# Spreading a batch norm's scale and shift over partitions: VectorE turns and quadrant copies in place of TensorE matmuls

## The chip, the core and the metric

The kernel runs on one core of one Trainium2 chip. The metric is the device time of one execution in microseconds; the time of a kernel is the median of its runs.

## The reference

A matrix product of 8192 rows (16 x 512) by 1024 by 768 columns, then a batch norm over all rows of each column, all in float32:

```python
batch, m, k, n = 16, 512, 1024, 768
...
y = np.matmul(x, weight)
mean = np.mean(y, axis=(0, 1), keepdims=True)
var = np.var(y, axis=(0, 1), keepdims=True)
y_norm = (y - mean) / np.sqrt(var + eps)
return (gamma * y_norm + beta).astype(np.float32)
```

No output can be stored until the statistics of its column over all 8192 rows are known.

## The kernel before

The 8192 rows are cut into 16 chunks of 512 (`C = 16`, `CH = 512`), the 768 columns into 6 tiles of 128 (`NT = 6`). x is read as float32 and cast to bf16 by the Pool queue's DMAs (`load_x`, L403) into a ring; VectorE turns it (`turn_x`, L435) so that k lies on partitions.

The first two column tiles (`GA = 2`, together `NA = 256` columns) are computed in two ways. For chunks 0 to 13 the product has **rows on partitions** (`mm_rows`, L510): sums and squares are added up in the tiles `sum1`, `sum2` and `sum3`, and a bf16 copy of y is kept. For the last two chunks (`RC = 14`) it has **columns on partitions** (`ga_unit`, L814), with statistics by VectorE. The other four tiles have columns on partitions throughout (`mm`, L575), each with its own pass over the chunks; some of those passes' work is already done while x still arrives.

When all chunks of the first two tiles are through, their statistics are finished: `merge` and `more` (L795, L800) join the accumulators into `tot`; eight small matmuls (`sums_rows`, L871) sum over partitions; `sums_entry` and `aggregate_rows` (L880 to L887) give mean and variance; `root_rows` (L891) takes the root on ScalarE; `scale_rows` and `shift_rows` (L894 to L899) make scale and shift with one column on each partition. That form serves the blocks of chunks 14 and 15 (`ga_block`): VectorE normalises them in place (L1064), TensorE turns them (L1074), ScalarE copies them out of PSUM (L1082), SyncE stores them (L1085).

The blocks of chunks 0 to 13 (`rows_out`) need scale and shift along the free dimension, the same on every partition. In the kernel before, TensorE does that spread (`spread`, L903): a matmul of the scale column, broadcast, with a float32 identity, four times for scale and shift of two tiles, each of which shows as two matmuls in the profile; the results stay in two PSUM banks (`aff[0]`, `aff[1]`). `shift_sbuf` (L915) copies the shift to `sum1` for Pool, which can't read it in PSUM here. Then VectorE multiplies each block (L937), VectorE (the blocks in `ADDED`) or Pool adds the shift (both L942), and SyncE stores (L946).

While this goes on, TensorE continues with tile 2, whose statistics for chunks 4 to 15 are ScalarE's (`keep_sum` L720, `square_sum` L724), then with tiles 3, 4 and 5, whose statistics are VectorE's (L711). Three of these tiles have some blocks (`raw_block`) whose scale and shift are spread in another way: `raw_spread` makes the two columns 32 wide, turns them in 32 x 32 blocks on VectorE (L1142), gathers the four quadrants into the first one (`gather`, L1145), deals them to the other three quadrants, and keeps them in a bank (L1158).

The order of all this is not written out by hand. Every step is a `task` with a due time (`prio`), the engines that may run it with estimated costs, what it depends on, and the buffers that it takes. `arrange` simulates the engines with these estimates, and at each moment takes, among the tasks that can start, the one with the lowest due time. The order that comes out is fixed per engine when the kernel is built. TensorE can host transposes of finished blocks between the matmuls of a chunk (`hosts`). So a change of a cost or a due time can move work far from its place.

Of the kernel before, what the change touches and what calls it, by code (L numbers as in the profile page):

```python
# [227 lines left out]
def kernel(  # L228
# [19 lines left out]
    P = 128  # L248
    NT = N // P
    KQ = K // 4  # L250
    CH = 512
# [13 lines left out]
    GA = 2  # L265
    NA = GA * P
    GY = 2
    PAD = 50
    HELD = 1
    PAIRED = 1  # L270
    ASTAT = {2:tuple(range(4,16))}
    RC = C - 2
    XT, YB, SQ = C - EARLY, 28, 3
    ADDED = (0,6,16,28,40)
# [18 lines left out]
    def seq(bi):  # L293

        ins = bi.ins
        prev = last.get(ins.engine)
        if prev is not None:
            tc.add_manual_dep(
                ins, prev,
                mybir.DependencyInfo(mybir.DependencyClass.NoSync, mybir.DependencyReason.DATA),  # L300
                reason="order",
            )
        last[ins.engine] = ins.name
        return bi
# [26 lines left out]
        seq(nc.vector.memset(sums[nt][:, 1:2], float(len(ASTAT[nt]) * CH)))  # L331
    msq = singles.tile([P, GA], f32)
    gst = singles.tile([P, GA, 3 + 12 * (C - RC)], f32)
    seq(nc.vector.memset(gst, float(RC * CH)))
    ngamma = singles.tile([P, NT], f32)
    nscale = singles.tile([P, 1], f32)
# [19 lines left out]
    def task(prio, engines, emit, deps=(), lock=False, **kw):  # L356
        t = Task(prio, engines, emit, deps, **kw)
        t.lock = lock
        tasks.append(t)
        return t  # L360

    def dve(occ):
        return {"DVE": (occ, occ + 0.09)}

    def act(occ):
        return {"ACT": (occ, occ + 0.11)}

    def pool(occ):
        return {"POOL": (occ, occ + 0.05)}

    def pe(occ):
        return {"PE": (occ, occ + 0.03)}
# [73 lines left out]
    t = 1.0  # L446
# [412 lines left out]


    S = clock[0]
    tot_slot, a0_slot, a1_slot = Slot(banks), Slot(banks), Slot(banks)
    aff = {}

    def sums_rows(eng):
# [24 lines left out]
    def root_rows(eng):  # L890
        seq(nc.scalar.activation(std[:, g], mv[:, g, 1], AF.Sqrt, bias=eps_sb, scale=1.0))  # L891

    def scale_rows(eng):
        seq(nc.vector.reciprocal(std[:, g], std[:, g]))  # L894
        seq(nc.vector.tensor_mul(scale[:, g], std[:, g], gamma_sb[:, g]))

    def shift_rows(eng):
        seq(nc.vector.tensor_mul(tmp[:, g], mv[:, g, 0], scale[:, g]))
        seq(nc.vector.tensor_sub(shift[:, g], beta_sb[:, g], tmp[:, g]))  # L899

    def spread(dst, row, nt):

        seq(nc.tensor.matmul(dst, row[:, nt:nt + 1].to_broadcast([P, P]), ident32, start=True, stop=True,  # L903
                             skip_group_check=True))

    def spread_rows(i):
        def emit(eng):
            a_ps = psum.tile([P, CH], f32, tag="b")
            aff[i] = a_ps[:, 0:NA]
            for a in range(GA):  # L910
                spread(a_ps[:, a * P:(a + 1) * P], (scale, shift)[i], a)
        return emit

    def shift_sbuf(eng):
        seq(nc.scalar.copy(sum1[:, 0:NA], aff[1]))  # L915

    U = S - 30.0
    s1 = task(U, pe(0.9), sums_rows, merges, takes=[tot_slot])
    se = task(U, dve(0.8), sums_entry, [s1], True, uses=[tot_slot])
    ag = [task(U, dve(0.25), aggregate_rows(a), [se] + [h[0] for k, h in ga_half.items() if k[0] == a]) for a in range(GA)]  # L920
    rt = task(U, {"ACT": (0.2, 0.3)}, root_rows, ag)
    sc = task(U, dve(0.3), scale_rows, [rt], True)
    sr = task(U + 0.1, dve(0.35), shift_rows, [sc], True)
    p0 = task(U, pe(0.45), spread_rows(0), [sc], takes=[a0_slot])
    p1 = task(U, pe(0.45), spread_rows(1), [sr], takes=[a1_slot])
    p1.look = 0.6
    sh = task(U, act(0.3), shift_sbuf, [p1], uses=[a1_slot])


    def rows_out(c, s0, s1, k):  # L930
        due = S + 5.0 + 0.62 * k
        n = s1 - s0
        slot = Slot(rings, n * NA)

        def norm(eng):
            slot.o = piece(slot).rearrange("p (s n) -> p s n", n=NA)
            seq(nc.vector.tensor_mul(  # L937
                slot.o, y_row[c].y[:, s0:s1], aff[0][:, None, :].to_broadcast([P, n, NA])))

        def add(eng):  # L940
            row = sum1[:, 0:NA] if eng == "POOL" else aff[1]
            seq(ENG[eng].tensor_add(slot.o, slot.o, row[:, None, :].to_broadcast([P, n, NA])))  # L942

        def store(eng):
            m0 = c * CH
            seq(nc.sync.dma_start(  # L946
                out_flat[m0 + s0 * P:m0 + s1 * P, 0:NA].rearrange("(s p) n -> p s n", p=P), slot.o))

        keeps = [row_end[k][3] for k in row_end if k[0] == c]
        a = task(due, dve(0.3 * n), norm, [p0] + keeps, takes=[slot], uses=[y_row[c], a0_slot])  # L950
        b = task(due + 0.4, dve(0.3 * n) if k in ADDED else pool(0.59 * n), add, [a, p1 if k in ADDED else sh],
                 uses=[slot, a1_slot] if k in ADDED else [slot])
        task(due + 1.0, {"SP": (0.38, 0.4)}, store, [b], dma=n * NA * P * 4 / 1024 / 365.0 * 1.024,
             uses=[slot])

# [100 lines left out]
    def ga_block(c, due):  # L1056
        yslot = y_row[c]
        slot, bank = Slot(rings, RT * NA), Slot(banks)
        todo = []

        def norm_ga(a):
            def emit(eng):
                part = yslot.y[:, a]
                seq(nc.vector.tensor_scalar(  # L1064
                    part, part, scale[:, a:a + 1], shift[:, a:a + 1], op0=ALU.mult, op1=ALU.add))
            return emit

        def step():
            if not todo:
                o_ps = psum.tile([P, RT, GA, P], bf16, tag="b")  # L1070
                bank.tile = o_ps
                todo.extend((o_ps[:, s, a], yslot.y[:, a, s * P:(s + 1) * P]) for s in range(RT) for a in range(GA))
            dst, src = todo.pop(0)
            seq(nc.tensor.transpose(dst, src, ident))  # L1074

        def emit(eng):
            for _ in range(emit.task.count):
                step()

        def copy(eng):  # L1080
            slot.o = piece(slot).rearrange("p (s n) -> p s n", n=NA)
            seq(nc.scalar.copy(slot.o, bank.tile.rearrange("p s a n -> p s (a n)")))  # L1082

        def store(eng):
            seq(nc.sync.dma_start(out_flat[c * CH:(c + 1) * CH, 0:NA].rearrange("(s p) n -> p s n", p=P), slot.o))  # L1085

        emit.step = step
        norms = [task(due, dve(0.25), norm_ga(a), [sr] + [h[1] for k, h in ga_half.items() if k[1] == c], True, uses=[yslot])
                 for a in range(GA)]
        t = task(due, pe(0.0555 * RT * GA), emit, norms, takes=[bank], uses=[yslot])  # L1090
        emit.task = t
        turns[t] = [RT * GA, RT * GA]
        d = task(due, act(0.905), copy, [t], takes=[slot], uses=[bank])
        task(due, {"SP": (0.38, 0.4)}, store, [d], dma=RT * NA * P * 4 / 1024 / 365.0 * 1.024, uses=[slot])

    for c in range(RC, C):
        ga_block(c, S - 29.8 + 35.5 * (c - RC))

    def raw_turn(nt, c, due):

# [26 lines left out]
    def raw_spread(nt, fin_task):  # L1127
        bank = Slot(banks)
        k = sorted(RAW).index(nt)
        acc, at = ((sum2, 0), (sum2, 2 * P), (sum3, 2 * P))[k]  # L1130
        row = acc[:, at:at + 2 * P].rearrange("p (i n) -> p i n", n=P)
        wide, turned = sum1[:, NA + 64 * k:NA + 64 * (k + 1)], sum3[:, 64 * k:64 * (k + 1)]
        both = turned.rearrange("p (i n) -> p i n", n=32)
        now = clock[0] + RAWDUE[nt] + 2.0

        def quadrant(i):
            return slice(32 * i, 32 * i + 32)

# [24 lines left out]
        t = task(now, act(0.4), keep, [s], takes=[bank])  # L1163
        raw_aff[nt] = bank, t, s, row[:, 1]
# [247 lines left out]
```

## Time and profile before

| | us |
|---|---|
| median of 3 runs | 205.81 |
| lowest, highest | 205.71, 205.83 |
| span of the profiled execution (first to last instruction) | 204.1 |
| busy: TensorE, VectorE, ScalarE, Pool in that span | 189.3, 159.3, 146.2, 124.1 |
| HBM read, written | 36.71 MB, 25.17 MB |

The page and the trace give the profiled execution's time as its span; what lies around the span isn't recorded there separately, so it is read as the median less the span, 1.71 us. In the profile PE is TensorE, PEld its weight loads, DVE VectorE, ACT ScalarE, POOL GpSimd (Pool), SP SyncE, which issues the stores. The first x arrives at about 12 us; the statistics of the first two tiles are complete at about 106 us, and the stores begin at 109 us.

### The profile page before, as it was taken

What the parts mean: (1) busy time and instruction counts of PE and PEld (TensorE: products, weight loads), DVE (VectorE), ACT (ScalarE), POOL (GpSimd) and SP (SyncE); (2) the same over time, 40 slices, a digit from 0 to 9 for tenths busy, and PEclk for the clock granted to TensorE, in tenths of its full rate; (3) what the DMA queues carried; (4) which work ended last, traced back from release to release, by engine and by line L of the source; (5) the groups of instructions that cost most, each with busy time, mean ns of one, the idle gap of its engine ahead of it and who ended that gap; (6) DMA issues with size and microseconds to landing.
All of it is one profiled execution on the core that took longest, in us unless ns stands there. A gap on an engine that the chain in (4) does not pass through costs nothing.

```text
span 204.1 us, 3510 instructions
## 1 busy us (share of the span) xinstructions
PE 189.3 (93%) x1210; PEld 114.5 (56%) x1210; DVE 159.3 (78%) x250; ACT 146.2 (72%) x260; POOL 124.1 (61%) x150
## 2 busy tenths in 40 slices
PE   7969999999999999999999999999999999997900
PEld 3457554657488888777865444444444445544600
DVE  4031879999999999969989998987999878657900
ACT  2001461368989999899978766999998959956950
POOL 7776954877499989997403999389613312940000
PEclk9999999999999999999999999999999999999965
DMA  4999999999999999999686899899999999999998
GB/s 71 172 199 196 176 196 196 196 197 197 190 193 197 197 196 196 196 197 195 103 181 200 297 339 336 248 301 328 295 322 227 336 303 274 347 343 310 310 347 253
DMA packets 98562, 48.74 MB, mean 239 GB/s; under 512 B 24304, under 2 KB 98032, under 8 KB 98544
## 3 DMA queue, kind: packets, MB, share of 16 engines
q0 software_dynamic: 34624, 18.36, 65.5%
q1 hardware_dynamic: 63920, 30.16, 52.6%
q8 instruction: 9, 0.15, 0.3%
q14 instruction: 9, 0.07, 0.1%
HBM read 36.71 MB, written 25.17 MB: 303 GB/s over the span
## 4 chain that ended last, share of the span: by engine, by line
PE 86%; ACT 3%; DMA 3%; POOL 2%; issue 1%; ACTq 0%; DVE 0%; POOLq 0%
PE y_ps L575 54%; PE y_ps L510 24%; PE y_ps L814 4%; ACT o_sb L1361 3%; DMA ring<-in_x_dram 3%; PE o_ps L1044 1%; POOL ring L403 1%; POOL w_sb L387 1%; PE y_ps L753 1%; PE a_ps L903 1%; PE o_ps L1074 0%; ACTq L1407 0%; PE idle_ps L591 0%; PE tot_ps L871 0%; ACT ring L1252 0%
## 5 line engine op out<-in xcount | busy, mean ns | idle before, releaser
L575 PEld LDWEIGHTS <-w_sb 128*128 128x128 bf16 x520 | 50.3, 97 | 57.6
L575 PE MATMUL y_ps<-xT_sb,w_sb 128*128 128x512 bf16 (+1 forms) x272 | 59.3, 371 | 0.0
L575 PE MATMUL y_ps<-x_pl,w_sb 128*128 128x512 bf16 x248 | 57.4, 379 | 0.0
L403 POOL DMA_DIRECT2D ring<-in_x_dram x76 | 47.2, 626 | 14.4 <-DMA ring<-in_x_dram 5.5
L510 PE MATMUL y_ps<-w_sb,xT_sb 128*128 128x256 bf16 x448 | 50.6, 273 | 1.7 <-DMA ring<-in_x_dram 1.6
L510 PEld LDWEIGHTS <-xT_sb 128*128 128x128 bf16 x448 | 43.5, 98 | 9.4 <-DVE xT_sb L435 2.9
L435 DVE STREAM_TRANSPOSE xT_sb<-ring 128x1024 f32<-128x1024 f32 (+1 forms) x29 | 31.2, 1111 | 14.1 <-DMA ring<-in_x_dram 13.9
L711 DVE BATCH_NORM_STATS2 stats<-y_ps 128x6 f32<-128x512 f32 x46 | 30.9, 687 | 7.7 <-PE y_ps L575 7.2
L715 ACT CAST y_sb<-y_ps 128x512 bf16<-128x512 f32 x51 | 29.0, 593 | 10.4 <-DVE stats L711 6.3
L547 ACT COPY x_pl<-xT_sb 128x1024 bf16<-128x1024 bf16 x32 | 32.8, 1063 | 1.7 <-DVE xT_sb L435 1.7
L942 POOL TENSOR_TENSOR ring<-ring,sum 128x1024 f32<-128x1024 f32 (+1 forms) x11 | 23.8, 2188 | 14.9 <-ACT y_ps L724 10.9
L659 ACT ACTIVATE sq_sb<-y_ps 128x512 f32<-128x512 f32 x28 | 16.3, 610 | 16.2 <-PE y_ps L510 15.9
L666 POOL TENSOR_TENSOR sum<-sum,sq_sb 128x512 f32<-128x512 f32 x20 | 25.6, 1278 | 3.0 <-ACT sq_sb L659 1.7
L662 DVE TENSOR_TENSOR sum<-y_ps,sum 128x512 f32<-128x512 f32 x28 | 18.9, 675 | 6.3 <-ACT sq_sb L659 5.3
L672 ACT CAST y_sb<-y_ps 128x512 bf16<-128x512 f32 x28 | 16.3, 594 | 8.2 <-DVE sum L662 8.0
L1178 POOL TENSOR_TENSOR ring<-ring,sum 128x1024 f32<-128x1024 f32 x6 | 14.8, 2477 | 9.8 <-issue 8.5
L937 DVE TENSOR_TENSOR ring<-y_sb,a_ps 128x1024 f32<-128x1024 bf16 (+1 forms) x16 | 16.7, 1079 | 0.1
L1044 PE MATMUL o_ps<-ident,y_sb 128*128 128x128 bf16 x104 | 13.1, 221 | 1.6 <-DVE y_sb L1348 1.5
L1232 ACT CAST ring<-ring 128x1024 f32<-128x1024 bf16 x13 | 13.8, 1063 | 0.6 <-DMA ring<-y_sb 0.6
L1145 POOL COPY sum<-sum 32x256 f32<-32x256 f32 (+1 forms) x17 | 5.8, 340 | 13.4 <-DVE sum L1142 6.5
L428 DVE STREAM_TRANSPOSE xT_sb<-ring 128x2048 bf16<-128x2048 bf16 x6 | 13.5, 2290 | 0.1
L591 PE MATMUL idle_ps<-idle_sb 128*128 128x512 f32 x18 | 9.6, 688 | 1.5 <-DVE idle_sb L316 1.5
(104 smaller groups left out, 153.7 us busy)
## 6 DMA issues: line engine op xcount, KB each, us to landing
out_dram<-ring SPq DMA_DIRECT2D x37, 512.0 KB, 3.4
ring<-in_x_dram POOLq DMA_DIRECT2D x52, 256.0 KB, 8.8
out_dram<-o_sb SPq DMA_DIRECT2D x6, 512.0 KB, 4.7
ring<-in_x_dram POOLq DMA_DIRECT2D x16, 128.0 KB, 5.9
w_sb<-in_weight_dram POOLq DMA_DIRECT2D x8, 192.0 KB, 6.2
out_dram<-ring SPq DMA_DIRECT2D x6, 256.0 KB, 3.0
ring<-in_x_dram POOLq DMA_DIRECT2D x4, 192.0 KB, 7.8
out_dram<-o_sb SPq DMA_DIRECT2D x3, 256.0 KB, 2.5
```

The lines of the kernel that those rows point to most:

```text
L403: bi = seq(nc.gpsimd.dma_start(x_bf[32 * i:32 * i + 32], src[:, :, KQ * i:KQ * (i + 1)]))
L435: seq(nc.vector.transpose(dst, src[:, :, jw0:jw1]))
L510: seq(nc.tensor.matmul(y_ps[:, s], x_of(c, jw, e, t * P, (t + 1) * P), w_sb[:, jw, e, 0:NA], start=(s == 0 and jw == 0 and e == 0), stop=( ...
L547: seq(nc.scalar.copy(dst, pairs) if eng == "ACT" else ENG[eng].tensor_copy(dst, pairs))
L575: seq(nc.tensor.matmul(y_ps, w_sb[:, jw, e, nt * P:(nt + 1) * P], moving(c, jw, e, q0 * QR, q1 * QR, parted), start=(jw == 0 and e == 0 an ...
L659: seq(nc.scalar.activation(sq_sb[:, 0:n], slot.tile[:, 0:n], AF.Square))
L662: seq(nc.vector.tensor_add(sum1, slot.tile[:, 0:n], sum1))
L666: seq(ENG[eng].tensor_add(acc, acc, state["sq"][:, 0:n]))
L711: seq(nc.vector.bn_stats(dst, slot.tile))
L715: seq(nc.scalar.copy(y(nt, c), slot.tile))
L937: seq(nc.vector.tensor_mul(slot.o, y_row[c].y[:, s0:s1], aff[0][:, None, :].to_broadcast([P, n, NA])))
L942: seq(ENG[eng].tensor_add(slot.o, slot.o, row[:, None, :].to_broadcast([P, n, NA])))
```

## The change

The four spreads on TensorE, `scale_rows`, `shift_rows` and `shift_sbuf` are gone. In their place: `terms_rows` (Pool) puts gamma, 0 and beta into two small tiles; `first_rows` (VectorE) makes -mean * gamma; `affine_rows` takes the reciprocal of the root and writes scale and shift of each tile 32 wide into `wide_rows`, a part of `sum2`; `turn_affine` turns them in 32 x 32 blocks into `sum3`; `gather_affine` (ScalarE, four copies) brings the quadrants together in the first 32 partitions of `sum1`; `deal_affine` copies these to the other three quadrants (VectorE or ScalarE); `keep_affine` copies the whole into one PSUM bank, where scale and shift now lie side by side. Pool reads the shift in `sum1`.

The blocks of chunks 14 and 15 take scale and shift from `wide_rows`. Both are now due ahead of the row blocks, where the second was due later; their copies out of PSUM may go to VectorE too. `raw_spread` uses another part of `sum1`, and a padding shrinks by the space of the two new tiles.

```diff
-    PAD = 50
+    PAD = 48
...
+    gcoef = singles.tile([P, GA, 2], f32)
+    gbase = singles.tile([P, GA, 2], f32)
...
-    tot_slot, a0_slot, a1_slot = Slot(banks), Slot(banks), Slot(banks)
+    tot_slot, aff_slot = Slot(banks), Slot(banks)
...
-    def scale_rows(eng):
+    wide_rows = sum2[:, 0:2 * GA * 32].rearrange("p (a i n) -> p a i n", i=2, n=32)
+    turned_rows = sum3[:, 0:2 * GA * 32].rearrange("p (a i n) -> p a i n", i=2, n=32)
+
+    def terms_rows(eng):
+        seq(nc.gpsimd.tensor_copy(gcoef[:, :, 0], gamma_sb[:, g]))
+        seq(nc.gpsimd.memset(gbase[:, :, 0], 0.0))
+        seq(nc.gpsimd.tensor_copy(gbase[:, :, 1], beta_sb[:, g]))
+
+    def first_rows(eng):
+        seq(nc.vector.scalar_tensor_tensor(
+            gcoef[:, :, 1], mv[:, g, 0], -1.0, gamma_sb[:, g], op0=ALU.mult, op1=ALU.mult))
+
+    def affine_rows(eng):
         seq(nc.vector.reciprocal(std[:, g], std[:, g]))
-        seq(nc.vector.tensor_mul(scale[:, g], std[:, g], gamma_sb[:, g]))
-
-    def shift_rows(eng):
-        seq(nc.vector.tensor_mul(tmp[:, g], mv[:, g, 0], scale[:, g]))
-        seq(nc.vector.tensor_sub(shift[:, g], beta_sb[:, g], tmp[:, g]))
-
-    def spread(dst, row, nt):
-
-        seq(nc.tensor.matmul(dst, row[:, nt:nt + 1].to_broadcast([P, P]), ident32, start=True, stop=True,
-                             skip_group_check=True))
-
-    def spread_rows(i):
+        for a in range(GA):
+            seq(nc.vector.scalar_tensor_tensor(
+                wide_rows[:, a], gcoef[:, a, :, None].to_broadcast([P, 2, 32]), std[:, a:a + 1],
+                gbase[:, a, :, None].to_broadcast([P, 2, 32]), op0=ALU.mult, op1=ALU.add))
+
+    def quad(i):
+        return slice(32 * i, 32 * i + 32)
+
+    def turn_affine(eng):
+        seq(nc.vector.transpose(sum3[:, 0:2 * GA * 32], sum2[:, 0:2 * GA * 32]))
+
+    def move_affine(eng, dst, src):
+        seq(nc.scalar.copy(dst, src) if eng == "ACT" else ENG[eng].tensor_copy(dst, src))
+
+    def gather_affine(eng):
+        row = sum1.rearrange("p (i a n) -> p a i n", a=GA, n=P)
+        for i in range(4):
+            move_affine(eng, row[0:32, :, :, quad(i)], turned_rows[quad(i)])
+
+    def deal_affine(i):
         def emit(eng):
-            a_ps = psum.tile([P, CH], f32, tag="b")
-            aff[i] = a_ps[:, 0:NA]
-            for a in range(GA):
-                spread(a_ps[:, a * P:(a + 1) * P], (scale, shift)[i], a)
+            move_affine(eng, sum1[quad(i)], sum1[0:32])
         return emit
 
-    def shift_sbuf(eng):
-        seq(nc.scalar.copy(sum1[:, 0:NA], aff[1]))
+    def keep_affine(eng):
+        a_ps = psum.tile([P, CH], f32, tag="b")
+        if eng == "ACT":
+            seq(nc.scalar.copy(a_ps, sum1))
+        else:
+            seq(nc.vector.tensor_copy(a_ps, sum1))
+        aff[0], aff[1] = a_ps[:, 0:NA], a_ps[:, NA:2 * NA]
...
-    sc = task(U, dve(0.3), scale_rows, [rt], True)
-    sr = task(U + 0.1, dve(0.35), shift_rows, [sc], True)
-    p0 = task(U, pe(0.45), spread_rows(0), [sc], takes=[a0_slot])
-    p1 = task(U, pe(0.45), spread_rows(1), [sr], takes=[a1_slot])
-    p1.look = 0.6
-    sh = task(U, act(0.3), shift_sbuf, [p1], uses=[a1_slot])
+    te = task(S - 20.0, pool(0.5), terms_rows, [affine_loads])
+    ft = task(U, dve(0.15), first_rows, ag, True)
+    sr = task(U, dve(0.6), affine_rows, [rt, ft, te] + merges, True)
+    tr = task(U, dve(0.25), turn_affine, [sr], True)
+    gt = task(U, {"ACT": (0.9, 1.0)}, gather_affine, [tr])
+    dl = [task(U + 0.05 * i, {"DVE": (0.6, 0.65), "ACT": (0.6, 0.7)}, deal_affine(i), [gt]) for i in range(1, 4)]
+    p0 = task(U, {"ACT": (0.6, 0.7), "DVE": (0.6, 0.7)}, keep_affine, dl, takes=[aff_slot])
...
-                    part, part, scale[:, a:a + 1], shift[:, a:a + 1], op0=ALU.mult, op1=ALU.add))
+                    part, part, wide_rows[:, a, 0, 0:1], wide_rows[:, a, 1, 0:1], op0=ALU.mult, op1=ALU.add))
...
-        d = task(due, act(0.905), copy, [t], takes=[slot], uses=[bank])
+        d = task(due, {"ACT": (0.905, 1.0), "DVE": (1.1, 1.2)}, copy, [t], takes=[slot], uses=[bank])
...
-        ga_block(c, S - 29.8 + 35.5 * (c - RC))
+        ga_block(c, S - 29.9 + 0.1 * (c - RC))
...
-        wide, turned = sum1[:, NA + 64 * k:NA + 64 * (k + 1)], sum3[:, 64 * k:64 * (k + 1)]
+        wide, turned = sum1[:, 64 * k:64 * (k + 1)], sum3[:, 64 * k:64 * (k + 1)]
```

Left out: the row of `rows_out`'s Pool add, now `sum1[:, NA:2 * NA]`, and the renamed slots and dependencies that follow from the one bank.

More of the change, by code (lines that the diff above doesn't have):

```diff
@@ L940, in add @@
         def add(eng):
-            row = sum1[:, 0:NA] if eng == "POOL" else aff[1]
+            row = sum1[:, NA:2 * NA] if eng == "POOL" else aff[1]
             seq(ENG[eng].tensor_add(slot.o, slot.o, row[:, None, :].to_broadcast([P, n, NA])))
@@ L949, in rows_out @@
         keeps = [row_end[k][3] for k in row_end if k[0] == c]
-        a = task(due, dve(0.3 * n), norm, [p0] + keeps, takes=[slot], uses=[y_row[c], a0_slot])
-        b = task(due + 0.4, dve(0.3 * n) if k in ADDED else pool(0.59 * n), add, [a, p1 if k in ADDED else sh],
-                 uses=[slot, a1_slot] if k in ADDED else [slot])
+        a = task(due, dve(0.3 * n), norm, [p0] + keeps, takes=[slot], uses=[y_row[c], aff_slot])
+        b = task(due + 0.4, dve(0.3 * n) if k in ADDED else pool(0.59 * n), add, [a, p0] if k in ADDED else [a] + dl,
+                 uses=[slot, aff_slot] if k in ADDED else [slot])
         task(due + 1.0, {"SP": (0.38, 0.4)}, store, [b], dma=n * NA * P * 4 / 1024 / 365.0 * 1.024,
@@ L1081, in copy @@
             slot.o = piece(slot).rearrange("p (s n) -> p s n", n=NA)
-            seq(nc.scalar.copy(slot.o, bank.tile.rearrange("p s a n -> p s (a n)")))
+            part = bank.tile.rearrange("p s a n -> p s (a n)")
+            seq(nc.scalar.copy(slot.o, part) if eng == "ACT" else nc.vector.tensor_copy(slot.o, part))
         def store(eng):
```

## The prediction

> **What bounds the kernel now.** I read the engine totals first, then the 40 slices, then the chain of waits, then the order of time around the place that changes, then busy time by stage.
>
> ```profile
> PE 189.3 (93%) x1210; PEld 114.5 (56%) x1210; DVE 159.3 (78%) x250; ACT 146.2 (72%) x260; POOL 124.1 (61%) x150
> PE   7969999999999999999999999999999999997900
> DVE  4031879999999999969989998987999878657900
> PEclk9999999999999999999999999999999999999965
> ```
>
> TensorE leaves no slice open from about 20 us to the end of the matmuls, at full granted clock. A busy row alone isn't proof of a bound; the chain shows the pace:
>
> ```profile
> 96.87 2.72 PE y_ps L814 x24
> 99.60 0.78 PE tot_ps L871 x8
> 100.38 4.56 PE y_ps L814 x40
> 104.94 1.73 PE y_ps L575 x8
> 106.66 1.05 PE a_ps L903 x8
> 107.72 0.51 PE o_ps L1074 x8
> 108.23 1.73 PE y_ps L575 x8
> 109.95 0.45 PE o_ps L1074 x8
> 110.40 58.94 PE y_ps L575 x269
> ```
>
> Eight matmuls of 512 columns take 1.73 us, 0.216 us each, in pairs of chunks on both sides of the place, and the 269 from 110.4 us take 0.219 each: the stream runs at one rate and nothing lies between its pieces. The line to see is the fifth: the eight spreads L903 cost 1.05 us of that stream, with nobody else's work in it. After the stream come 2 us of last statistics, then the last tile's stores.
>
> Now what the other resources have to spare after that place (each row: the stage, its length, busy us of PE, PEld, DVE, ACT and POOL, granted clock, DMA share, GB/s):
>
> ```profile
> 107.60:110.20 2.60, 2.60 (x26) 1.60 (x24) 2.49 (x7) 2.31 (x5) 0.00 (x0) 1.00 0.23 61
> 110.20:123.00 12.80, 12.80 (x62) 5.53 (x60) 12.70 (x14) 9.81 (x30) 12.07 (x7) 1.00 0.93 327
> 123.00:135.00 12.00, 12.00 (x56) 5.30 (x55) 10.91 (x15) 10.40 (x23) 8.46 (x4) 1.00 0.90 275
> 135.00:144.00 9.00, 9.00 (x43) 4.00 (x42) 7.01 (x12) 9.00 (x14) 8.19 (x11) 1.00 1.09 329
> 144.00:171.00 27.00, 27.00 (x132) 12.39 (x130) 24.17 (x52) 23.06 (x38) 7.94 (x11) 1.00 1.19 301
> 186.00:192.00 6.00, 4.43 (x54) 3.07 (x51) 5.22 (x19) 5.10 (x12) 0.00 (x0) 1.00 0.95 284
> ```
>
> VectorE is full from 110 to 123 us (12.70 of 12.80), has 1.09 us open in 123 to 135 and 1.99 in 135 to 144, and 2.83 in the 27 us after. Stores are nearly full from 144 us on. In 195 to 201 us they run at 347 GB/s; at 284 in 186 to 192 us they leave 6 x (1 - 284/347) = 1.09 us.
>
> **The change, part by part.** The sum is made against the profiled span, 204.1 us; the median run is 205.81, so 1.71 us lie around the span and are taken as fixed.
>
> Removed from TensorE: the four spreads of scale and the four of shift, 1.05 us on the chain. Nothing takes their place there. -1.05.
>
> The new chain starts where the old one did, when the root L891 ends at 106.05 us. Reciprocal 0.17 (L894). Two scalar_tensor_tensor of 128x64: between 0.16 (L898, 128x2) and 0.57 (L795 on VectorE, 128x256), by elements 0.26; two are 0.5. One transpose of 128x128: L1142 takes 0.245 for 64 columns, L435 1.11 for 1024, so 0.30. With gaps of 0.03 the turned rows stand at 107.15. ScalarE is then at its chunk of statistics until 107.23, so the four gathers of 32x128 start there: L1145 on ScalarE takes 0.24 for 64 elements, L1158 0.38 for 256, so 0.29, started 0.25 apart: 108.3. The three deals of 32x512 go to VectorE or ScalarE, two rounds. On ScalarE the same two rows drawn on to 512 give 0.56. On VectorE the bounds are 0.17 (L1141, 32 elements) and 0.68 (L662, 512 elements, two inputs); I take 0.5. They end at 109.45. The keep into the PSUM bank, 128x512, is a ScalarE copy like L715's 0.59: 110.05. The first row block's multiply, L937, starts at 110.1 in place of 107.59: 2.5 us later.
>
> The Trainium skill ("VectorE: DVE Perf Modes", The perf-mode tier table and its cycle sketch) has a float32 copy inside SBUF at two elements a cycle, from which I estimate (150 + 256)/0.96 = 0.42 us for a deal on VectorE. No copy of that shape is in this trace; by it the rows would begin 0.1 to 0.2 us sooner.
>
> What VectorE loses by that: of the four block normalisations L1064 (0.73 us for two) one pair ran after 107.59 and now fits into the wait, and so does the negated gamma (0.16). Lateness of the row stage on VectorE: 2.5 - 0.73 = 1.8 us. If the two block copies (L1082, 1.02 us each on ScalarE) go to VectorE, up to 2.0 more; a 128x1024 pass there takes 0.96 (L547) to 1.21 (L937). I take 1.8, since ScalarE frees up first for at least one of them and the other fits partly into the wait.
>
> Who waits for that: the row stores and the Pool adds (L942), whose first starts at 110.46 and would start about 112.2. VectorE has 1.09 + 1.99 = 3.08 us open by 144 us. TensorE's stream now asks for its statistics 1.05 us earlier, which leaves 2.03. So 1.8 fits, just. The statistics (L711) go ahead of the row blocks by their due times, so TensorE's banks aren't what is late; one bank holds both rows now where two did, so a bank more is free until 133 us.
>
> ScalarE: less 0.37 (L915), plus 1.05 of gathers, 0.56 to 1.1 of deals and 0.59 of keep, about +2.1 us. From 113 us it has 0.39 to 0.52 us open behind each of six chunks (its waits for y_ps in the listing by time), 3 us by 123: hidden. Each new step there waits in a queue served in order: behind the first gather, which waits for the transpose, and behind the keep, which waits for the last deal (1.1 us at most, if nothing is put between), stand the tile-2 statistics L720 and L724, and behind those TensorE's banks. A chunk fills one bank in 1.73 us, and by 105.8 us (the end of the last L827) the banks of the units before have been read, so several of the eight are free and the 2.1 us are covered; without that cover TensorE would stop for up to 2 us.
>
> Pool gets three small instructions (terms): L1318 to L1320 of the same kind take 0.34 together. If they stand ahead of the merges they delay them: L800 ends at 99.33 and the sums L871 begin at 99.43, so there is 0.1 of room, and matmuls are in order. Cost 0 to 0.34; Pool's queue also issues the x loads, but the last of those leaves at 95.4 and the last x transposes, 99.0 to 101.4, are on VectorE. I take 0.15.
>
> The two blocks with columns on partitions were normalised at 106.9 and 109.0 us and issued from 109.6 on; now both come ahead of all row blocks. On SyncE they pass the first row store (109.10), in a queue that has nothing else from 107 to 109 us. These stores (1 MB, 3 us at 347 GB/s) fill the write queue while the row stage is late, where the queue now idles at 61 GB/s. Same transposes on TensorE (0.96 for both), so 0 on the path. The padding is storage alone: 0.
>
> The end: stores pushed by the late row stage find room, as the DMA share of 0.90 in 123 to 135 us against 1.19 later is some 3 us open. If none are left over, the last tile's stores start 1.05 - 0.15 = 0.9 us earlier and the span ends with them. 204.1 - 0.9 + 1.7 = 204.9 us.
>
> **The rivals.** (a) The freed microsecond turns into a wait on TensorE: a transpose of a block queued behind a normalisation that is late (the planner counts 0.25 us for one, the row shows 0.41), a bank not freed, or the full 0.34 at the sums. Against it: at the same place today the stream waits for nothing. Price between 0.4 and 1.2 us of the gain: 205.2 to 206.0, mostly 205.6.
>
> (b) Slower: VectorE becomes the bound. Place: the row stage, 110 to 150 us. If deals, keep and both block copies go to VectorE ahead of the row blocks, the lateness is 1.8 + 2.0 = 3.8 us against 2.03 of room. The rest, 1.8 us, goes on into 143 to 150 us, where VectorE splits the late tiles (L547) that TensorE's next chunks read, and behind it into stores that are full. It decides against the change from 3.1 us of lateness on. 204.8 + 1.8 = 206.6 us. That point is the 2.03 us of room and the 1.05 of the gain. For it: the copies may choose VectorE now. Against it: ScalarE can take the same work, and 1.09 us of store room stands open at the end.
>
> (c) TensorE isn't the bound at all, so the spreads cost nothing. The share of weight loads, 56% of the span, speaks for it; the even 0.216 us per matmul and the gapless chain speak against. 205.8 us. The Trainium skill ("Perfetto Trace Analysis", Identifying the Most-Contended Engine) has matmul occupancy as a poor measure and the weight loads' share as the one to judge by; by that rule TensorE has headroom here and the gain would be none. Here the trace's rate per matmul decides against it.
>
> That the spreads might stay is excluded: the diff has no call of them left.
>
> **How the numbers follow.** Forecast 0.50, at 204.9; (a) 0.18; (b) 0.27; (c) 0.05. What counts as no change is within 0.2%, 0.41 us, about what a measurement of this kernel can tell: 205.4 to 206.2. Faster: the forecast and a quarter of (a), 0.55. Slower: (b) and a trace of (a), 0.28. Same: the rest, 0.17. The forecast's own range is 204.6 (no cost at the sums, 204.76, and the 0.1 us by which the runs before differ) to 205.3. The range over all goes to 206.6, the price of (b), leaving out half of (b) and a few of the forecast's low side.
>
> **What would show it.** Right: no a_ps on PE; L575 chunks still 1.73 us per eight with no gap between 104 and 112 us; the last-tile matmuls (L753) ending near 185.6 in place of 186.6; first L937 between 110 and 111 us; last L937 before 137. Wrong: a wait of PE on y_sb, on sum or on a DVE or ACT name between 99 and 150 us; L937 running past 138 us; x_pl copies later against their matmuls; more than 347 GB/s worth of stores queued at 186 us, so that the last store doesn't move.

## The result and the profile after

| | before | changed |
|---|---|---|
| median, us | 205.78 (4 runs) | 208.70 (4 runs) |
| lowest, highest | 205.71, 205.83 | 208.35, 208.98 |
| profiled execution, us (span) | 205.83 (204.1) | 208.35 (206.6) |

The ratio is 1.0141 [1.0124, 1.0158]: slower by 2.9 us, where 0.9 us less was forecast, and outside the range.

The changed kernel's page, with the same three rows as were shown of before, and the head of its chain of waits:

```profile
PE 190.2 (92%) x1202; PEld 115.6 (56%) x1202; DVE 161.5 (78%) x255; ACT 149.0 (72%) x273; POOL 121.5 (59%) x143
PE   7999999999999999999999999999999999995700
DVE  4031979989999899969989999879999995668500
PEclk9999999999999999999999999999999999999665
...
ACT 8%; PE 5%; DMA 3%; DVE 2%; issue 1%; ACTq 0%; POOL 0%; DVEq 0%
```

The totals hardly differ. The chain does: before, TensorE made up 86% of the span in it; now the chain can be followed back over some 19% of the span only, and that part passes through ScalarE, TensorE, DMA and VectorE in turn. What set the pace ahead of that part the chain doesn't show.

TensorE around the place that changed, in order of time (start, duration, engine, line, operation, count; in brackets, where there is one, the idle time before it):

```profile
104.83 3.61 PE L577 MATMUL y_ps<-x_pl,w_sb 128*128 128x512 bf16 x16
108.28 1.06 PE L1099 MATMUL o_ps<-ident,y_sb 128*128 128x128 bf16 x16
109.17 2.75 PE L577 MATMUL y_ps<-x_pl,w_sb 128*128 128x512 bf16 x12
```

The spreads are gone, and no line carries an idle time. But the order is another one: two chunks (16 matmuls) now run ahead of the transposes, where before one chunk and the spreads did. The stream stands about 1.0 us ahead from here on.

The new chain on VectorE:

```profile
106.13 0.17 DVE L908 RECIPROCAL std<-std 128x2 f32<-128x2 f32 x1 [0.17 <-ACT std L893]
106.42 0.48 DVE L910 SCALAR_TENSOR_TENSOR sum<-gcoef,std,gbase 128x64 f32<-128x64 f32 x2
107.00 0.31 DVE L918 STREAM_TRANSPOSE sum<-sum 128x128 f32<-128x128 f32 x1
107.24 1.34 DVE L1089 TENSOR_SCALAR y_sb<-y_sb,sum 128x512 bf16<-128x512 bf16 x4
108.50 0.17 DVE L989 TENSOR_SCALAR ngamma<-gamma_sb 128x6 f32<-128x6 f32 x1
108.68 0.85 DVE L921 COPY sum<-sum 32x512 f32<-32x512 f32 x2
109.63 0.69 DVE L938 COPY a_ps<-sum 128x512 f32<-128x512 f32 x1
110.36 0.69 DVE L962 TENSOR_TENSOR ring<-y_sb,a_ps 128x512 f32<-128x512 bf16 x1
```

All four normalisations and the negated gamma fit into the wait for ScalarE's gathers, and the first row multiply starts at 110.36 us. Up to here the forecast describes the run.

By stage (columns as before: the stage, its length, busy us of PE, PEld, DVE, ACT, POOL, granted clock, DMA share, GB/s):

```profile
107.60:110.20 2.60, 2.60 (x25) 1.68 (x24) 2.47 (x8) 2.51 (x7) 0.00 (x0) 1.00 0.79 121
110.20:123.00 12.80, 12.80 (x58) 5.46 (x57) 12.63 (x15) 11.42 (x40) 10.05 (x6) 1.00 0.81 287
123.00:135.00 12.00, 12.00 (x56) 5.30 (x55) 10.81 (x15) 10.43 (x16) 8.95 (x4) 1.00 1.02 298
135.00:144.00 9.00, 9.00 (x43) 4.03 (x42) 8.21 (x14) 8.11 (x18) 5.29 (x4) 1.00 1.01 304
144.00:171.00 27.00, 26.76 (x129) 12.16 (x127) 26.15 (x53) 24.02 (x41) 8.67 (x8) 1.00 1.16 301
171.00:174.00 3.00, 3.00 (x24) 1.70 (x23) 1.28 (x3) 3.00 (x5) 1.19 (x3) 1.00 0.52 153
174.00:186.00 12.00, 12.00 (x78) 6.67 (x77) 7.82 (x12) 8.34 (x12) 6.24 (x3) 1.00 1.16 341
186.00:192.00 6.00, 3.48 (x41) 2.50 (x38) 5.34 (x19) 5.10 (x13) 0.83 (x1) 0.92 1.15 345
```

The last column tells it. Before, 186 to 192 us ran at 284 GB/s, with about 1 us of room; now the writes run at 341 to 345 from 174 us on, so the end is the moment when the queue of stores is empty. What was not stored by 174 us can't be caught up any more, but for the room that the kernel before leaves unused. And two stages lag: 110 to 123 us (287 GB/s, before 327) and 171 to 174 us:

```profile
171.00:174.00 3.00, 3.00 (x24) 1.69 (x22) 2.72 (x4) 3.00 (x5) 0.91 (x3) 1.00 0.92 248
```

That is the row of before: 248 GB/s where the changed kernel has 153.

Adding up the packets of SyncE's queue (stores, and the transposes by DMA that it also carries) gives the megabytes landed by a time:

| us | 120 | 135 | 145 | 155 | 165 | 170 | 175 | 185 | 192 |
|---|---|---|---|---|---|---|---|---|---|
| before | 4.63 | 8.83 | 12.13 | 15.29 | 17.91 | 19.53 | 20.97 | 24.40 | 26.45 |
| changed | 3.83 | 8.53 | 11.47 | 14.66 | 17.48 | 19.07 | 20.14 | 23.55 | 25.96 |
| behind | 0.80 | 0.30 | 0.66 | 0.63 | 0.43 | 0.46 | 0.83 | 0.85 | 0.49 |

So the stores are late, in three steps: the late rows (0.80 MB, of which all but 0.30 is made good by 135 us), something between 135 and 145 us, and something between 170 and 175 us. The 0.83 MB at 175 us would be 2.4 us at 345 GB/s, close to the 2.5 by which the spans differ, but that agreement is in part chance. From 186 to 192 us the kernel before runs below the full rate, and the changed kernel makes good 0.36 MB; the 0.49 MB left are 1.4 us. The other 1.1 us lie at the very end: at 202 us the changed kernel has 0.74 MB to land, 2.1 us at 346 GB/s, but the last bytes land at 205.3 us, those behind 204 us at 69 GB/s and less, where the kernel before lands its last 0.25 MB at the full rate, by 202.8 us. Why the last bytes trickle isn't shown; all the grafts below do the same (0.7 to 1.0 us), the kernel before and `spread_cut` hardly (0.1 and 0.3 us).

TensorE's lead reaches the end of the matmuls (L755, the former L753, begins at 183.97 in place of 184.64) and is worth nothing there: the last statistics on VectorE stand behind a multiply (L1200) that waits 1.74 us for a store to free SBUF, and the first of the last tile's stores goes at 189.80 us, before at 189.31.

### The profile page after: what moved, and what is told of

Its sections match the earlier page's. It is cut to its first block, busy times and chain, and to the rows that moved or that the text cites. A ratio compares the mean times of both kernels' runs of the same rounds, so it can differ in the third digit from the quotient of the medians.

```text
span 206.6 us, 3499 instructions
## 1 busy us (share of the span) xinstructions
PE 190.2 (92%) x1202; PEld 115.6 (56%) x1202; DVE 161.5 (78%) x255; ACT 149.0 (72%) x273; POOL 121.5 (59%) x143
## 5 line engine op out<-in xcount | busy, mean ns | idle before, releaser
L713 DVE BATCH_NORM_STATS2 stats<-y_ps 128x6 f32<-128x512 f32 x46 | 30.0, 682 | 5.7 <-PE y_ps L577 5.7
L549 ACT COPY x_pl<-xT_sb 128x1024 bf16<-128x1024 bf16 x31 | 31.6, 1059 | 1.9 <-DVE xT_sb L437 1.7
L717 ACT CAST y_sb<-y_ps 128x512 bf16<-128x512 f32 x51 | 28.4, 593 | 4.8 <-DVE stats L713 3.1
L674 ACT CAST y_sb<-y_ps 128x512 bf16<-128x512 f32 x28 | 16.2, 597 | 8.1 <-DVE sum L664 7.8
L1069 PE MATMUL o_ps<-ident,y_sb 128*128 128x128 bf16 x104 | 13.8, 248 | 2.5 <-DVE y_sb L1374 2.5
L593 PE MATMUL idle_ps<-idle_sb 128*128 128x512 f32 x18 | 10.7, 753 | 1.5 <-DVE idle_sb L316 1.5
L1171 POOL COPY sum<-sum 32x64 f32<-32x64 f32 (+1 forms) x7 | 3.0, 433 | 15.3 <-ACT sum L1171 8.7
```

The source lines that it names most:

```text
L549: seq(nc.scalar.copy(dst, pairs) if eng == "ACT" else ENG[eng].tensor_copy(dst, pairs))
L713: seq(nc.vector.bn_stats(dst, slot.tile))
L717: seq(nc.scalar.copy(y(nt, c), slot.tile))
```

## The experiments

Ratios are to the kernel before on the same chip, whose median was between 205.68 and 206.07 us on the chips used; intervals are 95%.

**What the spreads cost TensorE.** `spread_cut`: the kernel before, in its own order, with a quarter of the spreads' matmuls.

```diff
-            for a in range(GA):
-                spread(a_ps[:, a * P:(a + 1) * P], (scale, shift)[i], a)
+            seq(nc.tensor.matmul(a_ps[:, 0:NA], ident, w_sb[:, 0, i, 0:NA], start=True, stop=True, ...))
```

> The kernel before in its own order, with the eight float32 passes of the spreads replaced by two bf16 matmuls of 256 columns (the rows' scale and shift are thereby other values). Asks what TensorE's microsecond is worth when nothing else changes. TensorE does 1.05 - 0.22 = 0.83 us less and the row blocks start up to 0.8 us sooner. If TensorE's stream is the bound: 205.8 - 0.8 = 205.0 us. If the store queue is the bound whatever TensorE does: 205.6 to 205.8, unless the earlier rows help it.

Measured: 206.03 us, 1.0008 [0.9996, 1.0021]. Its TensorE in order of time:

```profile
105.93 0.38 PE L910 MATMUL a_ps<-w_sb,ident 128*128 128x256 bf16 x2
106.77 0.89 PE L1074 MATMUL o_ps<-ident,y_sb 128*128 128x128 bf16 x8 [0.46 <-DVE y_sb L1064]
107.49 1.89 PE L575 MATMUL y_ps<-x_pl,w_sb 128*128 128x512 bf16 x8
```

The kernel before, in the same place:

```profile
106.87 0.73 DVE L1064 TENSOR_SCALAR y_sb<-y_sb,scale,shift 128x512 bf16<-128x512 bf16 x2
107.55 0.67 PE L1074 MATMUL o_ps<-ident,y_sb 128*128 128x128 bf16 x8
108.06 1.89 PE L575 MATMUL y_ps<-x_pl,w_sb 128*128 128x512 bf16 x8
```

The spreads take 0.38 us in place of two listings of 0.68 and 0.61. What follows is the bracket: TensorE now sits idle for 0.46 us until VectorE has normalised the block that the next transposes read, and those take 0.89 in place of 0.67 as they wait for its second half. In this execution the stream was 0.57 us ahead before the place already (in the listing, five of the matmuls L814 fewer were left at 103.75 us), and the next chunk starts at 107.49, which is 108.06 of before less 0.57: at the place itself nothing is left of the gain. The spreads had filled a wait, and the lines of the kernel before allow it to be seen: VectorE has the first half normalised at about 107.3 us (one half takes 0.41) and the second at 107.6, and the transposes start at 107.55.

**The two halves of the change apart.** `old_order_new_chain`: the new spread in the order of before, second block behind the row blocks. The tasks of before carry the new work, this one the deals and the keep:

```diff
     def shift_sbuf(eng):
-        seq(nc.scalar.copy(sum1[:, 0:NA], aff[1]))
+        seq(nc.scalar.copy(sum1[quad(1)], sum1[0:32]))
+        for j in (2, 3):
+            seq(nc.vector.tensor_copy(sum1[quad(j)], sum1[0:32]))
+        a_ps = psum.tile([P, CH], f32, tag="b")
+        seq(nc.vector.tensor_copy(a_ps, sum1))
```

> The new spread (turn, gathers, deals, keep) put into the order of the kernel before: each engine's list is that of before, but for the spread's own instructions. Theory 1, late rows: the row blocks start some 2.3 us later than before, their stores fall behind by 0.7 to 0.8 MB by 120 us, the store queue has no room to make that up, and the end is 207.5 to 208.7 us. Theory 2, the order: what costs is how the planner arranged the work after 130 us (tile 3's spread on ScalarE, the transposes' places on SyncE), so with the old order the 1.0 us of TensorE comes through: 204.8 to 205.5 us.

Measured: 210.21 us, 1.0209 [1.0172, 1.0245]. Its TensorE:

```profile
108.72 0.89 PE L1098 MATMUL o_ps<-ident,y_sb 128*128 128x128 bf16 x8 [0.88 <-DVE y_sb L1088]
109.45 1.89 PE L577 MATMUL y_ps<-x_pl,w_sb 128*128 128x512 bf16 x8
113.13 1.16 PE L1098 MATMUL o_ps<-ident,y_sb 128*128 128x128 bf16 x8 [1.80 <-DVE y_sb L1088]
114.09 2.34 PE L577 MATMUL y_ps<-x_pl,w_sb 128*128 128x512 bf16 x5
```

This mixes two things: the second block's normalisation stands behind the late rows on VectorE, and TensorE, served in order, stands still for it. Its stream is 5.3 us late from 118 us on. 1.2 of that it had well ahead of the place already in this execution, the slowest of four; the other 4.1 us, 2.7 of them the two waits in brackets, are about what the median is late (4.35). So it doesn't price the late rows; it shows that the new spread needs both blocks ahead of the rows, and that a TensorE so late is not made good.

`new_order_old_chain`: the changed kernel's order, with the eight matmuls back in it.

```diff
     def affine_rows(eng):
...
+        for i in range(2):
+            for a in range(GA):
+                seq(nc.tensor.matmul(aff[i][:, a * P:(a + 1) * P], (scale, shift)[i][:, a:a + 1]..., ident32, ...))
...
     def turn_affine(eng):
-        seq(nc.vector.transpose(sum3[:, 0:2 * GA * 32], sum2[:, 0:2 * GA * 32]))
+        pass
```

> The old TensorE spreads put into the order of the changed kernel: each engine's list is that of the changed kernel, but for the spread's own instructions. TensorE does 1.05 us more than in the changed kernel, the row blocks start at about 108.5 us in place of 110.4 (107.6 before). Theory 1, late rows: 206 to 207 us, faster than the changed kernel in spite of TensorE's work. Theory 2, the order: as slow as the changed kernel or slower, 208.5 to 209.7 us.

Measured: 209.53 us, 1.0178 [1.0148, 1.0207], though the rows start sooner. So the loss doesn't hang on the new spread: without it, in the same order, the kernel is no faster. By the medians it is even 0.8 us slower than the changed one (the intervals just overlap); whether that is TensorE's microsecond, which might count in this order, isn't shown.

`new_order_no_copies`: the changed kernel with gathers and deals left out.

```diff
-            move_affine(eng, row[0:32, :, :, quad(i)], turned_rows[quad(i)])
+            pass
...
-            move_affine(eng, sum1[quad(i)], sum1[0:32])
+            pass
```

> The changed kernel in its own order without the four gathers and the three deals (scale and shift of the row blocks are thereby wrong; the keep stays). TensorE's work is that of the changed kernel; ScalarE and VectorE do 1.9 and 0.9 us less, and the row blocks start near 109.3 us. Theory 1, late rows: 206 to 207 us. Theory 2, the order: 208.3 to 208.7 us.

Measured: 208.42 us, 1.0124 [1.0100, 1.0148], the changed kernel's ratio within the intervals. At 120 us it had landed 4.28 MB (changed 3.83, before 4.63), but 10.26 at 140 and 20.17 at 175, as the changed kernel (10.31, 20.14): rows that start sooner lose that again by 140 us.

**Late rows or the later order.** `graft` has the changed kernel's own order up to the first row multiply and from there on the order of before, task for task and engine for engine. The list GIVEN is what `arrange` made of the kernel before:

```diff
+FROM = 337
+GIVEN = [[0,"POOL",[]],[59,"PE",[]],...]
...
+        forced = forced or tasks[FROM].end is not None
...
+        if forced:
+            at = dict((number[u], (u, r)) for u, r in seen if r is not None)
+            for j, j_engine, j_hosted in GIVEN:
+                if j in at:
+                    t, r = at[j]
+                    e, given = j_engine, dict(j_hosted)
+                    start = start_of(t, r, e)
+                    break
```

> The changed kernel whose order is its own up to the first row block's multiply and from there on the order of the kernel before (engine, place and hosted turns of each step). Theory of the order: what costs the 2.9 us is where the planner puts the later steps, above all the last row multiplies (139.8 us in the changed kernel, 133.5 before), behind which SyncE's stores stand in line. Then this kernel has its last row multiply at 134 to 137 us and takes 204.9 to 206.0 us. Theory of the late start: the row blocks begin at 110.4 us as in the changed kernel, so it stays at 207.5 to 208.7 us.

Measured: 206.45 us, 1.0037 [1.0017, 1.0058]. The same new spread, the same late start of the rows (110.1 us), and about three quarters of the loss is gone. Stages of graft:

```profile
171.00:174.00 3.00, 3.00 (x25) 1.71 (x23) 2.83 (x4) 3.00 (x5) 1.16 (x3) 1.00 1.19 329
174.00:186.00 12.00, 12.00 (x75) 6.41 (x73) 7.49 (x12) 8.34 (x13) 6.61 (x3) 1.00 1.15 345
186.00:192.00 6.00, 4.43 (x55) 2.97 (x53) 5.50 (x19) 5.20 (x12) 0.00 (x0) 1.00 1.08 326
```

It is 0.69 MB behind at 120 us as well, but only 0.11 at 175, as 171 to 174 us run at 329 GB/s. This is the room that the prediction counted on; it is there in the order of before.

`old_blocks_first`: the kernel before with the diff's due time of the two blocks alone.

```diff
-        ga_block(c, S - 29.8 + 35.5 * (c - RC))
+        ga_block(c, S - 29.9 + 0.1 * (c - RC))
```

> The kernel before with one edit: both blocks with columns on partitions due ahead of the row blocks; the old spreads stay, and the planner arranges again (six steps change their engine, some 25 places differ). Theory of the order: small reorder, last row multiply at 134 to 136 us, 205.6 to 206.8 us. Theory that blocks first is what costs: 207 us or more.

Measured: 206.36 us, 1.0027 [1.0014, 1.0040]: that half of the change costs a little by itself and is not the loss.

`new_rows_sooner`: the changed kernel with the row blocks due sooner, so that VectorE makes up for the late start.

```diff
-        due = S + 5.0 + 0.62 * k
+        due = S + 2.0 + 0.5 * k
```

> The changed kernel with the row blocks due sooner (S + 2 + 0.5 k in place of S + 5 + 0.62 k), arranged again by the planner, so that row multiplies pass later statistics on VectorE. Theory of the order, by way of the last row multiply: it comes at 134 to 137 us in place of 139.8, and the time falls to 205.5 to 207 us. If the late rows are not what costs: 208 to 209 us.

Measured: 208.00 us, 1.0103 [1.0071, 1.0135]. The row multiplies by length (min/median/max in ns) and by first and last start:

```profile
L962 DVE TENSOR_TENSOR ring<-y_sb,a_ps x16: 680/1214/1221, 110.3 to 132.5; 128x1024 f32<-128x1024 bf16 x12, 128x512 f32<-128x512 bf16 x4
```

The last one starts at 132.5 us, sooner than before's 133.5 (139.8 in the changed kernel), and the kernel is still a per cent slow. That alone doesn't clear the late rows, as the new due times make another order again, and the same two numbers slow the kernel before as well (`old_rows_sooner`, below); `graft_152` settles it.

`new_pool_spread`: the changed kernel with the later tiles' gathers and deals held on Pool, where they were before (three of them had gone to ScalarE).

```diff
-        g = task(now, {"POOL": (0.8, 0.85), "ACT": (0.9, 1.0)}, gather, [d])
-        s = task(now, {"POOL": (1.2, 1.25), "ACT": (1.0, 1.1)}, deal, [g])
+        g = task(now, {"POOL": (0.8, 0.85), "ACT": (0.9, 1.0)} if nt == NT - 2 else pool(0.8), gather, [d])
+        s = task(now, pool(1.2), deal, [g])
```

> The changed kernel with the later tiles' gathers and deals held on Pool as in the kernel before (three of them had moved to ScalarE), arranged again. If the moves to ScalarE are what costs (the pause of TensorE at 159.4 us and the late casts behind them): 206 to 207.5 us. If the late row blocks are: 208 to 209 us, with the last row multiply still at 139 us or later.

Measured: 208.46 us, 1.0119 [1.0093, 1.0144]. Little or nothing of the loss hangs on that.

`old_rows_sooner` is the control: the kernel before, all its work unchanged, with the same two due numbers changed.

> A control: the kernel before with its old spreads, all its work unchanged, and only the row blocks' due times moved (S + 2 + 0.5 k), so that the planner arranges 127 places anew, about as many as the change did (149). If it is being rearranged that costs, whatever for, because the due times and costs of the later steps were settled on the old order: 207 to 208.5 us. If the changed kernel's order is bad only by its late row blocks: these come sooner here than before, so 205.4 to 206.2 us.

Measured: 208.28 us, 1.0116 [1.0083, 1.0149]. With no other work at all, another order can cost about as much as the whole change does.

**Where in the order.** More grafts, which go over to the order of before later (at 137, 152 and so on): only FROM differs.

> The changed kernel with its own order up to tile 2's turned scale (137 us), from there on the order of before. If the loss is made by the order before 137 us (the late row blocks): 208 to 209 us. If it is made by the order after that: 206 to 207 us, as with the order of before from 111 us on (206.45).

> The same with its own order up to tile 3's turned scale (154 us). If the loss is made between 154 us and the end (tile 3's and tile 4's spreads on ScalarE, the store queue that runs dry at 171 to 174 us): 206 to 207 us. If it is made between 137 and 154 us (last row blocks, the queue's gap at 141 to 144 us): 207.5 to 209 us.

> The changed kernel with its own order up to tile 4's statistics (165 us), from there on the order of before. If most of the loss is made between 154 and 165 us (tile 3's deal on ScalarE, TensorE's pause at 159.4 us, the changed splits of the late chunks): 208 us or more. If it is made after 165 us (ScalarE's conversions and the store queue that runs dry at 171 to 174 us): 206.8 to 207.5 us, as with the order of before from 154 us on.

> The same with its own order up to tile 4's turned scale (169 us). If the queue that runs dry at 171 to 174 us is made by steps placed before that point (the conversions and statistics on ScalarE from 165 to 170 us): 208 us or more. If by the steps behind it: 206.8 to 207.5 us.

> The changed kernel as it is, on the same chip as the two that follow: 208.2 to 208.9 us, 1.4% over the kernel before.

| own order until (us) | median, us | ratio |
|---|---|---|
| first row multiply (graft) | 206.45 | 1.0037 [1.0017, 1.0058] |
| 137 | 207.51 | 1.0076 [1.0049, 1.0104] |
| 154 (graft_152) | 207.27 | 1.0049 [1.0024, 1.0073] |
| 165 (graft_164) | 206.91 | 1.0063 [1.0046, 1.0080] |
| 169 | 207.13 | 1.0073 [1.0056, 1.0090] |
| the end (new_again) | 208.21 | 1.0125 [1.0108, 1.0143] |

The grafts from 137 to 169 us can't be told from each other; the step behind 169 us can, half a per cent, and it was measured on one chip with the last three rows.

The row stage of graft_152 runs as the changed kernel's does, from 110.3 to 139.8 us (there 110.4 to 139.8):

```profile
L981 DVE TENSOR_TENSOR ring<-y_sb,a_ps x16: 677/1204/1222, 110.3 to 139.8; 128x1024 f32<-128x1024 bf16 x12, 128x512 f32<-128x512 bf16 x4
```

It loses 0.49% in place of 1.25 to 1.41. So rows that run late are not the main cause.

Behind 169 us the traces of new_again and graft_169 differ in SyncE's queue. In new_again (start, time on the queue, line, operation):

```profile
167.46 1.65 SPq L1246 DMA_TRANSPOSE ring<-y_sb  x1
171.46 0.37 SPq L1228 DMA_DIRECT2D out_dram<-ring  x1
171.92 1.44 SPq L1246 DMA_TRANSPOSE ring<-y_sb  x1
173.46 3.89 SPq L1228 DMA_DIRECT2D out_dram<-ring  x4
```

and in graft_169:

```profile
167.56 1.65 SPq L1265 DMA_TRANSPOSE ring<-y_sb  x1
169.31 0.54 SPq L1247 DMA_DIRECT2D out_dram<-ring  x1
169.94 1.65 SPq L1265 DMA_TRANSPOSE ring<-y_sb  x1
171.96 4.25 SPq L1247 DMA_DIRECT2D out_dram<-ring  x3
```

From 169.1 (167.46 + 1.65) to 171.46 us nothing leaves SyncE in new_again. The queue is served in order, and its next entry is a store that waits for a conversion on ScalarE, which there comes behind the gathers and a bank of another tile; this is its line:

```profile
170.39 1.05 ACT L1258 CAST ring<-ring 128x1024 f32<-128x1024 bf16 x1
```

In graft_169 ScalarE's conversion (L1277) comes before those gathers, at 168.06 us, its store leaves at 169.31, and the last transpose follows at once. What that makes of the stores, first new_again, then graft_169:

```profile
171.00:174.00 3.00, 3.00 (x25) 1.71 (x24) 0.93 (x2) 3.00 (x6) 0.88 (x2) 1.00 0.61 181
```

```profile
171.00:174.00 3.00, 3.00 (x24) 1.70 (x23) 1.86 (x3) 2.77 (x4) 1.16 (x3) 1.00 1.18 320
```

181 against 320 GB/s; by 175 us graft_169 is 0.58 MB ahead (20.82 against 20.24), 1.7 us at 345 GB/s. Of that 1.0 us reaches the spans (206.3 and 205.3): behind 174 us its stores run at 328 GB/s against 341. The gap is shown; that it is the whole of the half per cent is read off the traces and not tried by itself.

**A shorter spread.** `graft_fast`: graft with two of the four gathers on Pool and the keep in two halves.

```diff
-            move_affine(eng, row[0:32, :, :, quad(i)], turned_rows[quad(i)])
+            move_affine("ACT" if i < 2 else "POOL", row[0:32, :, :, quad(i)], turned_rows[quad(i)])
...
-            seq(nc.vector.tensor_copy(a_ps, sum1))
+        seq(nc.vector.tensor_copy(a_ps[:, 0:NA], sum1[:, 0:NA]))
+        seq(nc.scalar.copy(a_ps[:, NA:2 * NA], sum1[:, NA:2 * NA]))
```

> The changed kernel with the order of before from the first row block on (206.45 us) and a shorter spread: two of the four gathers on Pool, the keep in two halves on VectorE and ScalarE side by side. The rows should begin at 109.5 us in place of 110.1. If the rest over the kernel before (0.37%) comes from the rows' late start, by which stores are 0.8 MB behind at 120 us: 205.9 to 206.3 us. If not: 206.4 us again.

Measured: 207.38 us, 1.0064 [1.0041, 1.0087]. A miss: ScalarE's half of the keep waited for VectorE's half and the first multiply for both, so the rows began at 110.11 us as in graft. It says nothing on the price of the late rows. But it has the order of before and rows that begin when graft's do, and still lies 0.27% above graft's ratio, as high as the grafts from 137 us on; so a step of that size between two of these kernels can't be put down to their order. No version run here beats the kernel before.

## Why the prediction was wrong

- **The place itself: right.** Reciprocal 0.17, two scalar_tensor_tensor 0.48 for 0.5, turn 0.31 for 0.30, rows at 110.36 for 110.1, no gap on TensorE from 104 to 112 us, both block copies on ScalarE. The Trainium skill's estimate for a deal on VectorE ("VectorE: DVE Perf Modes", The perf-mode tier table and its cycle sketch) agrees: 0.42 us measured, where I took 0.5. The price of Pool's terms, 0.15, was 0: they ran at 55.7 us.
- **"1.05 us of that stream, with nobody else's work in it": this step failed first.** Gapless is not the same as free of waits. The transposes next in TensorE's queue read what VectorE finishes at about 107.3 and 107.6 us, and the spreads lay in that wait: spread_cut made them 0.8 us shorter and the time did not move. The changed kernel has TensorE 1.0 us ahead only because a second chunk moved in front of the transposes. At the end of the matmuls that lead was 0.67 us and bought nothing, as the stores set the end: the last tile's first store, forecast 0.9 us earlier, left 0.49 us later.
- **"Stores pushed by the late row stage find room": right in graft, wrong in the kernel.** All but 0.30 of 0.80 MB was made good by 135 us as worked out, and in graft all but 0.11 by 175 us. In the changed kernel 0.36 MB were lost again by 145 us and 0.37 from 170 to 175 us.
- **What the sum left out was the largest term.** It priced the tasks that the diff names and took the rest of the order as given. But `arrange` makes the order anew: 149 later places differ and 8 tasks change engine. Of the 1.25 to 1.41% lost, 0.37% is left when the order of before is put back (graft), so about 1.0% is rearrangement, or some 0.7% going by graft_fast, which kept 0.64; old_rows_sooner loses 1.16% with no other work at all. Half a per cent of it arises behind 169 us, with SyncE's queue dry for 2.4 us.
- **What stays open.** The rest, between 111 and 169 us, stays open, and with graft and graft_fast 0.27% apart it isn't clear that there is one. One candidate shows in the trace: from 140.6 to 143.5 us SyncE waits for the last row store behind Pool's add, and 141 to 144 us run at 226 GB/s, before at 286. But graft_169 has the same thin stretch (224 GB/s) and has landed 20.82 MB by 175 us, graft, which hasn't, 20.86: there it had been made good. Open as well is what makes up graft's 0.37%. Late rows, and a TensorE that waits for 0.7 us at 168 us, stand in its trace; but by 192 us it has landed 26.58 MB, more than the kernel before (26.45), and in the profiled execution it ends later only by the slow last bytes.
- **Rival (a)** had the wait for a late normalisation: spread_cut shows it (0.46 us), the changed kernel doesn't, as its second chunk runs in that time.
- **Rival (b)** had the sign, and at 206.6 came nearest, but its mechanism is at most a small part: it has VectorE's lateness pass into late stores, and graft_152, whose rows run as late as the changed kernel's, loses 0.49%. new_rows_sooner (rows that end sooner than before's, 1.03%) and new_order_no_copies (rows that start 1.2 us sooner, 1.24%) point the same way. Both block copies, which (b) feared for VectorE, ran on ScalarE.
- **Rival (c)** had the spreads' worth right. The Trainium skill's rule ("Perfetto Trace Analysis", Identifying the Most-Contended Engine; the page names the MFU beside the weight loads' share) gave no gain, and spread_cut's 1.0008 agrees, by way of the wait at that place. I had set the even rate per matmul against it; that shows a stream at its rate, not what its next instruction would otherwise wait for. But it isn't that TensorE has slack everywhere: in old_order_new_chain the 4.1 us that it lost at the place went through to the end.
- **Signs.** Of those named as "right", the spreads gone, no gap and the first row multiply came true; the last-tile matmuls ended at 185.95 us, between the 185.6 named and the 186.6 of before; the last row multiply started at 139.84 us, past the 138 named as wrong. That sign was misleading: graft_152 has it too. The last sign named as wrong was the telling one: from 186 to 192 us the stores run at 345 GB/s, nearly the 347 taken as full, and the last store comes later, not sooner.

## What to carry to other kernels

Before a stretch of work is priced as a gain, look at what the next instruction of the same queue waits for, and when that is ready: only the time beyond it is freed. Where a planner makes the order, a local edit is also a reordering of all that follows; replay the old order behind the edit, and shift a due time without any edit, and the two prices come apart. Where stores run at their full rate to the end, add up bytes landed by time in both kernels, up to the point from which both run at that rate: here the deficit there explains 1.4 of 2.5 us, and the times at which it grows lead to the entry in the in-order queue that waits ahead of others.

## What the runs showed of the hardware

- Float32 copies of 32x512 from one quadrant to another took 0.42 us on VectorE and 0.62 on ScalarE; 32x128 took 0.30 on ScalarE. From SBUF into a PSUM bank, 128x512 took 0.69 on VectorE.
- Two engines that each write one half of the same PSUM bank went one after the other in this build (graft_fast: VectorE's half ran from 109.24 to 109.67 us, ScalarE's began at 109.70).
- A transpose by DMA stood on SyncE's queue for 1.3 to 2.9 us (1.69 us median of 13, changed kernel). In new_again one store that wasn't ready kept the next of them, and the stores behind it, back for 2.4 us.
